# A fused LoRA linear layer on one core: the sixth chunk held back for the third store, and a self-test taken out

## The chip, the cores and the metric

The kernel runs on one core of one Trainium2 chip. The metric is the device time of one execution in microseconds (us); lower is better. A time is the median over several runs, and for this kernel 0.2% of it is 0.33 us. The profile shows one execution. Times inside it are microseconds from the start of its span. PE is TensorE (its weight loads are shown apart, as PEld), DVE is VectorE, ACT is ScalarE, POOL is GpSimd, SP is SyncE, which here only issues DMAs and waits.

## What is computed

`x` is 16 x 2048 x 256 in float32, so 32,768 rows of 256 values. `W` is 256 x 256, `lora_A` 256 x 16, `lora_B` 16 x 256, `lora_E` 16, `scale` is 1.

```python
y = x_flat @ W
lora_out = x_flat @ lora_A
lora_out = lora_out * lora_E
lora_out = lora_out @ lora_B
y = y + scale * lora_out
```

`x` is 33.55 MB, and so is the result. Both go through the core's 16 DMA engines once.

## The kernel before

The two low-rank factors are folded into the weight first: `weff = W + A E B`, a matrix of 256 x 256 in bf16 (lines 155 to 175). What is left is one product `x @ weff`.

**Chunks.** The rows are cut into nine chunks (`PLAN`, line 5), numbered 0 to 8: chunk 0 and chunk 6 have 16 rows per partition (2 MB), the others 32 rows (4 MB). There are six buffers in SBUF (`SLOTS`), and chunk i lives in buffer i mod 6. A chunk is loaded into its buffer, its result overwrites it there, and the buffer is stored to the output. So chunks 6, 7 and 8 use the buffers of chunks 0, 1 and 2 again.

**Steps.** Each chunk is worked off in steps of 8 rows per partition, 32 steps in all, t = 0 to 31. Chunk 0 is steps 0 and 1, chunk 1 is 2 to 5, chunk 2 is 6 to 9, chunk 3 is 10 to 13, chunk 4 is 14 to 17, chunk 5 is 18 to 21, chunk 6 is 22 and 23, chunk 7 is 24 to 27, chunk 8 is 28 to 31. A step goes through four engines' hands:

- DVE rounds the 8 rows to bf16 (`rounded(t)`, line 148; I write R(t)). Before the first step of a chunk it waits for that chunk's load (line 147).
- PE transposes them, two bf16 values as one 32-bit word (`transposed`, line 188; T(t)), into PSUM.
- DVE copies the transposed words to SBUF (`copied(t)`, line 152; C(t)).
- PE multiplies with `weff` (`multiplied`, line 197; M(t)), two groups of 4 rows, and ACT copies each group from PSUM over the input rows in the buffer (line 216).

**The order of each engine** is written out. DVE does R(0), R(1), and then C(t), R(t+2) for t = 0, 1, 2 and so on (lines 171 to 180). A DVE instruction that waits therefore holds up all behind it: R(18) stands between C(16) and C(17). PE does T(t+1), M(t) in a hardware loop (lines 205 to 208). ACT works in the order of the steps.

**The order of the DMAs** is that of SP. Ahead of everything come `W` and the loads of chunks 0 to 5 (lines 102 to 107). Then SP waits for each chunk in turn to be written by ACT, and issues its store (lines 224 and 225). After store 2 it issues loads 6, 7 and 8, each behind a wait until the store that used the same buffer (0, 1, 2) has landed (`AFTER`, lines 226 to 228). Store 3 is issued only behind load 8, then stores 4 to 8. ACT issues the three small loads of `lora_A`, `lora_B`, `lora_E`.

**The self-test** (lines 118 to 141) checks that a transpose of 32-bit words moves all bits unchanged: POOL makes two number patterns (`probe`, `want`), DVE shifts them, PE transposes one, DVE compares with the other and adds up the differences in `err`, which is 0. `err` is then added into `weff` (line 175), so `weff` waits for the test.

Of the kernel before, what the change touches and what calls it, by code (L numbers as in the profile page):

```python
# [7 lines left out]
LEAD = 6  # L8
AFTER = {2: [6, 7, 8]}

S, G = 8, 4
P = 128
FP32 = mybir.dt.float32
BF16 = mybir.dt.bfloat16
I32 = mybir.dt.int32


class Count:
# [12 lines left out]
def kernel(tc, x, W, lora_A, lora_B, lora_E, scale, out):  # L31
    nc = tc.nc
# [17 lines left out]
    def sbuf(name, shape, dt):  # L50
        return nc.alloc_sbuf_tensor(name, shape, dt).ap()

    def psum(name, shape, dt):
        return nc.alloc_psum_tensor(name, shape, dt).ap()
# [4 lines left out]
    w_sb = sbuf("w_sb", [P, KC, M], FP32)  # L59
# [3 lines left out]
    weff = sbuf("weff", [P, KC, M], BF16)  # L63
    ident = sbuf("ident", [P, P], FP32)
# [6 lines left out]
    ps_xt = [psum(f"psum_xt{k}", [P, S, P], FP32) for k in range(2)]  # L71
# [3 lines left out]
    ps_aeb = ps_xt[1][:, S // 2:, :].rearrange("p s t -> p (s t)").rearrange("p (c m) -> p c m", c=KC)  # L75

    s_w, s_a, s_b, s_e = (Count(nc, f"s_{k}") for k in "wabe")
    s_ld = [Count(nc, f"s_ld{i}") for i in range(len(PLAN))]
    s_st = [Count(nc, f"s_st{i}") for i in range(len(PLAN))]
    s_id, s_set, s_v, s_t, s_m, s_y = (  # L80
        Count(nc, k) for k in ("s_id", "s_set", "s_v", "s_t", "s_m", "s_y"))
# [3 lines left out]
    def slot(i):  # L85
        return slots[i % LEAD][:, :PLAN[i], :]
# [7 lines left out]
    def spent(engine, count):  # L94
        engine.wait_ge(count.sem, count.total).then_inc(count.sem, -count.total)
# [5 lines left out]
    with tc.tile_critical(no_gpsimd_drain=True):  # L101
# [12 lines left out]
        out=ident, in_=ident, compare_op=mybir.AluOpType.not_equal, fill=1.0, base=0,  # L114
        pattern=[[-1, P]], channel_multiplier=1))


    s_test = Count(nc, "s_test")
    probe = sbuf("probe", [P, P], I32)
    want = sbuf("want", [P, P], I32)  # L120
    got = sbuf("got", [P, P], FP32)
    s_test.by(nc.gpsimd.iota(probe, pattern=[[1, P]], base=0, channel_multiplier=P))
    s_test.by(nc.gpsimd.iota(want, pattern=[[P, P]], base=0, channel_multiplier=1))  # L123
    err = sbuf("err", [P, 1], FP32)
    A = mybir.AluOpType
    nc.vector.wait_ge(s_test.sem, 2)
    for t in (probe, want):
        s_test.by(nc.vector.tensor_scalar(out=t, in0=t, scalar1=16, scalar2=0x1235,  # L128
                                          op0=A.logical_shift_left, op1=A.bitwise_or))
    nc.tensor.wait_ge(s_test.sem, 4)  # L130
    nc.tensor.wait_ge(s_id.sem, 2)
    s_test.by(nc.tensor.transpose(ps_xt[0][:, 0, :], probe.bitcast(FP32), ident))  # L132
    nc.vector.wait_ge(s_test.sem, 5)
    s_test.by(nc.vector.tensor_copy(out=got, in_=ps_xt[0][:, 0, :]))  # L134
    nc.vector.wait_ge(s_test.sem, 6)
    s_test.by(nc.vector.tensor_tensor(out=want, in0=want, in1=got.bitcast(I32), op=A.bitwise_xor))  # L136
    nc.vector.wait_ge(s_test.sem, 7)
    s_test.by(nc.vector.tensor_scalar(out=got, in0=want, scalar1=0.0, scalar2=None, op0=A.not_equal))
    nc.vector.wait_ge(s_test.sem, 8)
    s_test.by(nc.vector.tensor_reduce(out=err, in_=got, axis=mybir.AxisListType.X, op=A.add))  # L140
    nc.tensor.wait_ge(s_test.sem, 6)


    def rounded(t):
        i, r = steps[t]
        if r == 0:
            nc.vector.wait_ge(s_ld[i].sem, 16)
        nc.vector.tensor_copy(out=xb[t % 2], in_=slot(i)[:, r:r + S, :]).then_inc(can_t, 1)  # L148

    def copied(t):  # L150
# [8 lines left out]
    for c in range(KC):  # L159
# [5 lines left out]
        out=ate, in0=ps_at, scalar1=e_sb, scalar2=float(scale),  # L165
        op0=mybir.AluOpType.mult, op1=mybir.AluOpType.mult))
    nc.tensor.wait_ge(s_v.sem, 2)
    for c in range(KC):
        aeb_done = nc.tensor.matmul(ps_aeb[:, c, :], ate[:, c, :], b_bf, start=True, stop=True)  # L169
    s_set.by(aeb_done)  # L170
    rounded(0)
    nc.vector.wait_ge(s_w.sem, 16)
    nc.vector.wait_ge(s_set.sem, 2)
    nc.vector.wait_ge(s_test.sem, 9)
    s_v.by(nc.vector.scalar_tensor_tensor(out=weff, in0=w_sb, scalar=err, in1=ps_aeb, op0=A.add, op1=A.add))  # L175
    rounded(1)
    for t in range(NS):
        copied(t)
        if t + 2 < NS:
            rounded(t + 2)  # L180
# [50 lines left out]
    for count in [s_a, s_id]:  # L231
        spent(nc.tensor, count)
    spent(nc.tensor, s_v)
    for count in [s_b, s_e, s_test, s_w, s_set, s_t] + s_ld:
        spent(nc.vector, count)
    spent(nc.scalar, s_m)
    nc.tensor.wait_ge(can_y, 1).then_inc(can_y, -1)
# [37 lines left out]
```

## Time and profile before

| | us |
|---|---|
| median of 3 runs | 163.13 (163.07 to 163.17) |
| the profiled execution, its own time | 162.98 |
| its span | 161.7 |
| outside the span | 1.3 |

| engine | busy us | share of the span | instructions |
|---|---|---|---|
| PE | 94.7 | 59% | 781 |
| PEld | 84.3 | 52% | 781 |
| DVE | 77.9 | 48% | 73 |
| ACT | 63.2 | 39% | 65 |
| POOL | 1.1 | 1% | 8 |

The DMA queue that SP feeds (q1) moved 67.37 MB, and its packets took 97.2% of the 16 engines' span. HBM was read for 33.85 MB and written for 33.55 MB, 417 GB/s over the span.

How to read it: a busy share is a mean over the whole span, and no compute engine is busy for more than 59% of it. What matters is which resource has no pause, and which of the waits in the order of SP and of DVE ends last. The profile has an answer that a page of shares does not print: the trace keeps a record of every DMA packet, with start, size and duration. For these big transfers a packet is 32,768 bytes (one partition of a 4 MB chunk) or 16,384 bytes (of a 2 MB chunk).

### The profile page before, as it was taken

To read this page: it belongs to the slowest core of one execution; us is meant where nothing else is said; L and a number is where in the kernel's file an instruction comes from. 1 tells how busy PE (TensorE), PEld (TensorE's weight loads), DVE (VectorE), ACT (ScalarE), POOL (GpSimd) and SP (SyncE) were. 2 spreads that over 40 slices of the span, in tenths; PEclk is the share of its full clock that TensorE was granted. 3 is DMA by queue.
4 is the path that set the end of the run, shared out by engine and by line. 5 is a ranking of instruction groups with operands and counts; after the bars stand their busy time and mean duration, and the time that the engine had idled before them with its cause. 6 is when DMAs were issued, how large, how long until landed. Compare 5 with 4: busy or idle time off the path is not lost. (4 is left out here: it accounts for less than half of the span.)

```text
span 161.7 us, 1984 instructions
## 1 busy us (share of the span) xinstructions
PE 94.7 (59%) x781; PEld 84.3 (52%) x781; DVE 77.9 (48%) x73; ACT 63.2 (39%) x65; POOL 1.1 (1%) x8
## 2 busy tenths in 40 slices
PE   0159399999999999994000895999995000000000
PEld 0037279999999999993000684999994000000000
DVE  0193297889898989860001907989840000000000
ACT  0300508686867767685000054677776000000000
POOL 0200000000000000000000000000000000000000
PEclk9999959999999999999755569999999655555555
DMA  4999999999999989999999999999999998999993
GB/s 138 430 454 454 414 430 454 422 422 454 422 430 446 399 341 446 454 446 397 462 385 450 462 438 399 454 438 397 478 422 405 462 438 381 478 438 397 462 438 146
DMA packets 2946, 67.42 MB, mean 417 GB/s; under 512 B 496, under 2 KB 512, under 8 KB 640
## 3 DMA queue, kind: packets, MB, share of 16 engines
q1 hardware_dynamic: 2736, 67.37, 97.2%
q10 hardware_dynamic: 208, 0.03, 0.2%
q14 instruction: 2, 0.02, 0.0%
HBM read 33.85 MB, written 33.55 MB: 417 GB/s over the span
## 5 line engine op out<-in xcount | busy, mean ns | idle before, releaser
L216 ACT COPY xy<-psum_y 128x1024 f32<-128x1024 f32 x64 | 61.9, 1017 | 55.8 <-PE psum_y L197 55.8
L197 PE MATMUL psum_y<-weff,xt 128*128 128x256 bf16 x512 | 64.9, 283 | 0.2 <-PEq L98 0.2
L197 PEld LDWEIGHTS psum_y<-weff,xt 128*128 128x128 bf16 x512 | 52.0, 102 | 7.7 <-issue 0.4
L148 DVE CAST xb<-xy 128x2048 bf16<-128x2048 f32 x32 | 39.0, 1219 | 27.3 <-DMA xy<-in_x_dram 27.3
L188 PE MATMUL psum_xt<-ident,xb 128*128 128x128 f32 x264 | 38.0, 293 | 20.2 <-PEq L98 20.2
L188 PEld LDWEIGHTS psum_xt<-ident,xb 128*128 128x128 f32 x264 | 32.9, 152 | 22.0 <-issue 21.6
L152 DVE COPY xt<-psum_xt 128x1024 f32<-128x1024 f32 x32 | 39.1, 1223 | 7.8 <-PE psum_xt L188 7.6
L132 PE MATMUL psum_xt<-ident,probe 128*128 128x128 f32 x1 | 0.5, 477 | 7.1 <-DVE want L128 7.1
L132 PEld LDWEIGHTS psum_xt<-ident,probe 128*128 128x128 f32 x1 | 0.2, 183 | 7.1 <-DVE want L128 7.1
L216 ACT ACT_TABLE_LOAD x1 | 1.3, 1283 | 5.7 <-PEq L109 5.7
L128 DVE TENSOR_SCALAR probe<-probe 128x128 int32<-128x128 int32 x1 | 0.2, 226 | 6.7 <-POOL want L123 6.7
L169 PE MATMUL psum_xt<-b_bf,ate 16*128 16x256 bf16 x2 | 0.6, 402 | 0.9 <-DVE ate L164 0.9
L169 PEld LDWEIGHTS psum_xt<-b_bf,ate 16*128 16x128 bf16 x2 | 0.1, 102 | 1.4 <-DVE ate L164 1.4
L160 PE MATMUL psum_xt<-ident,a_sb 128*16 128x128 f32 x2 | 0.6, 402 | 0.4 <-DVE got L134 0.4
L175 DVE SCALAR_TENSOR_TENSOR weff<-w_sb,err,psum_xt 128x512 bf16<-128x512 f32 x1 | 0.7, 742 | 0.0
L134 DVE COPY got<-psum_xt 128x128 f32<-128x128 f32 x1 | 0.3, 293 | 0.6 <-PE psum_xt L132 0.6
L164 DVE TENSOR_SCALAR ate<-psum_xt,e_sb 16x256 bf16<-16x256 f32 x1 | 0.5, 465 | 0.0
L160 PEld LDWEIGHTS psum_xt<-ident,a_sb 128*16 128x16 f32 x2 | 0.1, 92 | 0.7 <-DVE got L134 0.7
L136 DVE TENSOR_TENSOR want<-want,got 128x128 int32<-128x128 int32 x1 | 0.3, 292 | 0.0
L140 DVE TENSOR_REDUCE err<-got 128x1 f32<-128x128 f32 x1 | 0.3, 286 | 0.0
L113 POOL TENSOR_SCALAR_AFFINE_SELECT ident<-ident 128x128 f32<-128x128 f32 x1 | 0.3, 293 | 0.2 <-POOL ident L111 0.2
L156 DVE CAST b_bf<-b_sb 16x256 bf16<-16x256 f32 x1 | 0.3, 271 | 0.0
(9 smaller groups left out, 1.5 us busy)
## 6 DMA issues: line engine op xcount, KB each, us to landing
xy<-in_x_dram SPq DMA_DIRECT2D x7, 4096.0 KB, 26.6
out_dram<-xy SPq DMA_DIRECT2D x7, 4096.0 KB, 37.2
xy<-in_x_dram SPq DMA_DIRECT2D x2, 2048.0 KB, 16.1
out_dram<-xy SPq DMA_DIRECT2D x2, 2048.0 KB, 38.3
w_sb<-in_W_dram SPq DMA_DIRECT2D x1, 256.0 KB, 2.9
a_sb<-in_lora_A_dram ACTq DMA_DIRECT2D x1, 16.0 KB, 2.6
b_sb<-in_lora_B_dram ACTq DMA_DIRECT2D x1, 16.0 KB, 3.2
e_sb<-in_lora_E_dram ACTq DMA_DIRECT2D x1, 0.1 KB, 6.4
```

The source lines that it names most:

```text
L113: s_id.by(nc.gpsimd.affine_select(out=ident, in_=ident, compare_op=mybir.AluOpType.not_equal, fill=1.0, base=0, pattern=[[-1, P]], channel ...
L132: s_test.by(nc.tensor.transpose(ps_xt[0][:, 0, :], probe.bitcast(FP32), ident))
L134: s_test.by(nc.vector.tensor_copy(out=got, in_=ps_xt[0][:, 0, :]))
L148: nc.vector.tensor_copy(out=xb[t % 2], in_=slot(i)[:, r:r + S, :]).then_inc(can_t, 1)
L152: nc.vector.tensor_copy(out=xt[t % 2], in_=ps_xt[t % 2]).then_inc(can_m, 1)
L160: at_done = nc.tensor.transpose(ps_at[:, c, :], a_sb[:, c, :], ident)
L164: s_v.by(nc.vector.tensor_scalar(out=ate, in0=ps_at, scalar1=e_sb, scalar2=float(scale), op0=mybir.AluOpType.mult, op1=mybir.AluOpType.mult))
L169: aeb_done = nc.tensor.matmul(ps_aeb[:, c, :], ate[:, c, :], b_bf, start=True, stop=True)
L175: s_v.by(nc.vector.scalar_tensor_tensor(out=weff, in0=w_sb, scalar=err, in1=ps_aeb, op0=A.add, op1=A.add))
L188: done = nc.tensor.transpose(ps_xt[k][:, j, :], words[k][:, j, :], ident)
L197: done = nc.tensor.matmul(ps_y[h][:, j, :], pairs[k][:, h * G + j, :, c], weff[:, c, :], start=(c == 0), stop=(c == KC - 1))
L216: y = nc.scalar.copy(out=slot(i)[:, r:r + G, :], in_=ps_y[(n - 1) % 2])
```

## The change

It does two things.

1. `HOLD = {5: 2}`: before DVE rounds the first step of chunk 5 (that is R(18)), it waits, besides the load of chunk 5, until store 2 has landed.
2. The self-test is taken out: the two patterns on POOL, six instructions on DVE, one transpose on PE, and its semaphore. `weff` is now `W` plus the product, without `err`.

```diff
+HOLD = {5: 2}
...
-    s_test = Count(nc, "s_test")
-    probe = sbuf("probe", [P, P], I32)
-    want = sbuf("want", [P, P], I32)
-    got = sbuf("got", [P, P], FP32)
-    s_test.by(nc.gpsimd.iota(probe, ...))
-    s_test.by(nc.gpsimd.iota(want, ...))
...
-    for t in (probe, want):
-        s_test.by(nc.vector.tensor_scalar(out=t, in0=t, scalar1=16, scalar2=0x1235, ...))
...
-    s_test.by(nc.tensor.transpose(ps_xt[0][:, 0, :], probe.bitcast(FP32), ident))
...
-    s_test.by(nc.vector.tensor_copy(out=got, in_=ps_xt[0][:, 0, :]))
-    s_test.by(nc.vector.tensor_tensor(out=want, in0=want, in1=got.bitcast(I32), op=A.bitwise_xor))
-    s_test.by(nc.vector.tensor_scalar(out=got, in0=want, scalar1=0.0, scalar2=None, op0=A.not_equal))
-    s_test.by(nc.vector.tensor_reduce(out=err, in_=got, axis=mybir.AxisListType.X, op=A.add))
...
     def rounded(t):
         i, r = steps[t]
         if r == 0:
             nc.vector.wait_ge(s_ld[i].sem, 16)
+        if i in HOLD and r == 0:
+            nc.vector.wait_ge(s_st[HOLD[i]].sem, 16)
         nc.vector.tensor_copy(out=xb[t % 2], in_=slot(i)[:, r:r + S, :]).then_inc(can_t, 1)
...
-    nc.vector.wait_ge(s_test.sem, 9)
-    s_v.by(nc.vector.scalar_tensor_tensor(out=weff, in0=w_sb, scalar=err, in1=ps_aeb, op0=A.add, op1=A.add))
+    s_v.by(nc.vector.tensor_add(out=weff, in0=w_sb, in1=ps_aeb))
```

The order of the instructions on SP and ACT is the same in both kernels; on PE, DVE and POOL only the self-test's are missing, and the addition that makes `weff` is of another form.

More of the change, by code (lines that the diff above doesn't have):

```diff
@@ L14 @@
 BF16 = mybir.dt.bfloat16
-I32 = mybir.dt.int32
 class Count:
@@ L115 @@
         pattern=[[-1, P]], channel_multiplier=1))
-    s_test = Count(nc, "s_test")
-    probe = sbuf("probe", [P, P], I32)
-    want = sbuf("want", [P, P], I32)
-    got = sbuf("got", [P, P], FP32)
[L122 to L126, printed above, removed]
-    for t in (probe, want):
[L128 to L131, printed above, removed]
-    s_test.by(nc.tensor.transpose(ps_xt[0][:, 0, :], probe.bitcast(FP32), ident))
-    nc.vector.wait_ge(s_test.sem, 5)
-    s_test.by(nc.vector.tensor_copy(out=got, in_=ps_xt[0][:, 0, :]))
-    nc.vector.wait_ge(s_test.sem, 6)
-    s_test.by(nc.vector.tensor_tensor(out=want, in0=want, in1=got.bitcast(I32), op=A.bitwise_xor))
-    nc.vector.wait_ge(s_test.sem, 7)
-    s_test.by(nc.vector.tensor_scalar(out=got, in0=want, scalar1=0.0, scalar2=None, op0=A.not_equal))
-    nc.vector.wait_ge(s_test.sem, 8)
-    s_test.by(nc.vector.tensor_reduce(out=err, in_=got, axis=mybir.AxisListType.X, op=A.add))
-    nc.tensor.wait_ge(s_test.sem, 6)
     def rounded(t):
@@ L233 @@
     spent(nc.tensor, s_v)
-    for count in [s_b, s_e, s_test, s_w, s_set, s_t] + s_ld:
+    for count in [s_b, s_e, s_w, s_set, s_t] + s_ld:
         spent(nc.vector, count)
```

## The prediction, made before the changed kernel ran

> **What bounds the kernel now.** I read the slices of the page first, then SP's own waits, then the timeline, and last the packet records.
>
> ```profile
> PE   0159399999999999994000895999995000000000
> DVE  0193297889898989860001907989840000000000
> PEclk9999959999999999999755569999999655555555
> DMA  4999999999999989999999999999999998999993
> GB/s 138 430 454 454 414 430 454 422 422 454 422 430 446 399 341 446 454 446 397 462 385 450 462 438 399 454 438 397 478 422 405 462 438 381 478 438 397 462 438 146
> ```
>
> The DMA row has no pause from the second slice to the last but one. PE and DVE pause in slices 18 to 21, and from slice 31 on they do nothing. So the DMA engines set the end, although the chain of waits ends with ACT:
>
> ```profile
> 123.62 1.02 ACT xy L216
> ```
>
> Behind that copy, at 124.6, lie 37 us in which only stores run. The waits of SP tell that the transfers are a line, first in, first out:
>
> ```profile
> SPq L89 <- DMA out_dram<-xy: 35.3, 3, 16.8
> ...
> 64.12 19.63 SPq L89 DMA_DIRECT2D xy<-in_x_dram  x3
> 83.80 41.20 SPq L92 DMA_DIRECT2D out_dram<-xy  x6
> ```
>
> Load 6 is issued at 64.12, when store 0 has landed, and load 8 at 83.4, when store 2 has. By the records of the completion writes the landings are: load 5 59.3, stores 0 to 2 64.1, 73.8, 83.5, loads 6 to 8 88.4, 98.0, 107.8, stores 3 to 8 117.6, 127.7, 137.4, 142.3, 152.0, 161.6. Each transfer ends about 9.7 us (4 MB) or 4.9 us (2 MB) behind the one before, and the last landing is the end of the span.
>
> Then the packets. Of 1,792 packets of 32 KB, 1,650 took exactly 1,213 ns, and of 512 of 16 KB 466 took 611. Each DMA engine carries 112 and 32 of these: 135.9 + 19.6 = 155.4 us, with nothing lost. Joining each packet to the one that begins where it ended gives 16 unbroken chains, one per DMA engine. Fourteen end between 159.7 and 160.5, one at 161.03, one at 161.65. **The last one is the time.** Its packets over 1,213 ns, by stretch:
>
> ```
> stretch (us)    DMA does         compute runs   ns lost on the last chain / on the 14
> 10 - 53         loads            yes               9 / 5 to 25
> 53 - 57.9       end of load 5    yes             423 / 388 to 1308
> 57.9 - 76       stores 0, 1, 2   yes             821 / under 10
> 76 - 83.5       store 2          no              under 10 / under 10
> 83.5 - 106      loads 6, 7, 8    from 88         106 / under 20 (one 317)
> 106 - 126.5     stores 3, 4      to 124.6       1013 / under 10
> 126.5 - 161.6   stores 4 to 8    no              under 10 / under 10
> ```
>
> So one of 16 DMA engines is slower by some 72 ns in 1,213 (6%) whenever a store is moved while the compute engines run; not in loads, and not once they stop. It loses 0.82 + 1.01 us so, and comes in 0.62 us behind the next chain. That next one, at 161.03, lost about 1 us at the start and another at 57.0, where an 8 KB instruction fetch of 0.96 us lay between its packets.
>
> **The hold.** Before, R(18) began at 61.05; C(17) and all of chunk 5 went through by 75.8 (the last ACT copy there).
>
> ```profile
> 61.05 1.22 DVE L148 CAST xb<-xy 128x2048 bf16<-128x2048 f32 x1
> ...
> 63.40 1.93 ACT L216 COPY xy<-psum_y 128x1024 f32<-128x1024 f32 x2 [0.69 <-PE psum_y L197]
> ...
> 88.31 1.23 DVE L148 CAST xb<-xy 128x2048 bf16<-128x2048 f32 x1 [16.70 <-DMA xy<-in_x_dram]
> ```
>
> Now R(18) waits until store 2 lands, 83.5. Queued behind it on DVE is C(17), so step 17, the last of chunk 4, waits too, and store 4 with it. The last work ahead of the hold is step 16, whose ACT copies end at 63.40 + 1.93 = 65.3. Compute is silent from 65.3 to 83.5 in place of 75.8 to 88.3, and starts again just when loads 6 to 8 take over the DMA.
>
> *Saved under stores 0 to 2:* on the last chain the packets that begin at 65.5 and later lost 71, 61, 76, 71, 71, 71, 83 and 33 ns: 0.54 us.
>
> *Added under stores 3 and 4:* before, R(22) began cold at 88.31 and M(22) ended at 97.94. Moved to R(18) at 83.45, that is 4.86 us earlier and four steps back: M(18) ends at 93.08. From there the rows of the steady stretch give 2.62 us a step (0.87 of transposes and 1.75 of products, PE without a pause): M(31) ends at 93.08 + 13 x 2.62 = 127.1, and its copies 1.1 us later, 128.2, against 124.6. Loads 6 to 8 (88.4, 98.0, 107.8) are there before R(22), R(24), R(28) need them, at about 95, 100 and 111. So compute lies over the stores for 3.6 us more: 2.8 packets at 73 ns, the mean of the 13 whole packets there: 0.20 us.
>
> *The line of transfers:* step 17 done makes store 4 due at about 91, chunk 5's makes store 5 due at 102, store 6 at 107, store 7 at 118, store 8 at 128.2. The line reaches store 4 at 117.6, store 5 at 127.7 and store 8 at 152.0, so 24 us stay at the tightest, and order and bytes are unchanged. This backlog hides the later compute; without it each us of delay would be a us of time.
>
> *The sum:* -0.54 + 0.20 = -0.34 us on the last chain, which then ends at 161.3, still behind 161.03. What would be late next is that chain, so the hold can give 0.62 us at most.
>
> The Trainium skill speaks against this: "SBUF — State Buffer", section "SBUF: two separate sides", says engine ports and DMA ports are disjoint, and a DMA cannot be slowed by a compute op. The loads of 10 to 53 agree (1,213 ns under full compute); the 6% on one chain do not fit. By that rule they would come from elsewhere, and the hold would bring 0.
>
> **The self-test.** On DVE go 0.23 + 0.22 + 0.29 + 0.29 + 0.23 + 0.29 = 1.55 us, on PE one transpose of 0.48, on POOL 2 x 0.23. All of it runs between 6.3 and 8.9. R(0) began at 9.46, and load 0, issued at 1.38, takes 8.1 us (the shortest landing of L89): 9.5. So the load hides the test, and behind it R(2) waits 5.14 us for load 1 anyway. The plain addition has no row; it lies between 0.29 (a tensor op on 128 x 128) and 1.22 (a copy of 128 x 1024), and I take the 0.74 of the form that it replaces. The same wait hides each of them: 0. The bytes of W and x are the same. Fewer instructions can move the two fetches (57.0 and 100.5); they lie on two other chains, worth between 0 and 1 us there, and both end before 161.1. I take 0.
>
> **Result:** 162.98 - 0.34 = 162.64 on the profiled execution, and 163.13 - 0.34 = 162.8 on the median, which lies 0.15 above it.
>
> **The rivals.**
>
> 1. *No effect.* The 72 ns are not due to compute under stores, or are there only while the profile is recorded. For: it is one DMA engine of 16, while DVE, ACT and PE use all partitions alike, and records written for each instruction would stop with compute too. Against: the runs without its page take 163.07 to 163.17, not 0.6 us less than 162.98. Time: 163.13. This is what the page of the Trainium skill named above would give.
> 2. *The whole 0.54 and more.* If the extra 3.6 us cost nothing (the slow packets hang on an engine that is done early, as DVE is), the last chain falls to 161.1, to the limit of 161.03: 162.5 to 162.6.
> 3. *Slower by a bit.* The loss under stores 0 to 2 is of those stores and would come with an idle compute as well; then only the 0.20 remains. For: all of compute and those stores overlap, so the trace cannot part them. Against: 76 to 83.5, store 2 without compute, loses nothing. Time: 163.33, up to 163.5 if the continuous run costs twice as much a packet.
> 4. *Slower by much: the clock.* The granted clock was 0.5 from 78.9 to 96.0, and M(21) took 3.62 us cold against 1.91. My sum has as long a cold start (89.7 to 96.0, 6.3 us) from 84.8 on. Cold steps cost about 1.9 + 3.6 = 5.5 us, 2.9 more than warm. The 24 us of slack are used up by 8 more cold steps of the 14; each further one adds 2.9 us, and all 14 about 15 us: 178. Against: 26 steps in the trace run warm at 2.62 without a break.
>
> **How the numbers follow.** A measurement of this kernel tells about 0.2% (0.33 us) from no change, so the line for faster is 162.80 and my forecast lies on it; the price per packet (61 to 99 ns) and the end of compute (128.2 give or take 1) spread it from 162.6 to 163.0. Chances: forecast 0.62, of which 0.36 are beyond the line; no effect 0.17; rival 2 0.11; rival 3 0.07, of which 0.03 beyond 163.46; rival 4 0.03. Faster 0.36 + 0.11 = 0.47, slower 0.03 + 0.03 = 0.06, same 0.47. The range holds all but rival 4 and the outer ends: 162.4 to 163.35.
>
> **What would show it.** R(18) starts at 83.5, and DVE shows a wait of about 22 us for store 2 in place of 16.7 for load 6; ACT ends at about 128; SP issues store 4 at about 91 and store 5 at 102; on the last chain packets of 66 to 76 take 1,213 ns, and those of 106 to 129 some 1,285. Wrong if these stay slow while compute is silent, if slow packets appear under loads 6 to 8, or if a profile shows the 0.3 us and the runs do not.

## The result, and the profile after

The changed kernel takes 162.48 us (median of 11 runs, 162.40 to 162.91), against 163.05 before in the same series (162.87 to 163.29): a ratio of 0.9969, with an interval from 0.9960 to 0.9978. That is 0.51 us less (0.36 to 0.65). The profiled execution takes 162.47 with a span of 161.2, against 162.98 and 161.7.

The slices of the page, the same rows as before:

```profile
PE   0149089999999999000009999999999300000000
DVE  0164297898898982000049589899883000000000
PEclk9999969999999999955555899999999965555555
DMA  4999999999999989999999999999999998999993
```

The DMA row has the same digits as before. Counted from 0, the hole in PE and DVE has moved from slices 18 to 21 to slices 15 to 20, and behind it PE now runs on without the second dip that it had before. The end of the chain of waits and SP's issues:

```profile
126.40 1.02 ACT xy L192
```

```profile
63.50 19.67 SPq L90 DMA_DIRECT2D xy<-in_x_dram  x3
83.21 44.57 SPq L93 DMA_DIRECT2D out_dram<-xy  x6
```

Compute ends at 127.4 in place of 124.6, and the last store is issued 3 us later; 34 us of stores still follow, so that delay costs nothing. The hold itself, in DVE's timeline:

```profile
60.13 1.23 DVE L129 COPY xt<-psum_xt 128x1024 f32<-128x1024 f32 x1 [0.26 <-PE psum_xt L164]
82.92 1.23 DVE L125 CAST xb<-xy 128x2048 bf16<-128x2048 f32 x1 [21.57 <-DMA out_dram<-xy]
84.06 1.22 DVE L129 COPY xt<-psum_xt 128x1024 f32<-128x1024 f32 x1
```

The first row is C(16), the second R(18), released by a store's landing after 21.6 us, the third C(17), which had nothing left to wait for but its place in the line.

The packet records answer for the time. The chains are joined as in the prediction; the table has the ns lost over 1,213 (32 KB) and 611 (16 KB). All packet times, there and here, are set 0.50 us later than the trace has them, so that the last packet ends with the span.

```
                         before   after
last chain ends at       161.65   161.15
under stores 0 to 2         826     270
from store 3 on            1008    1260
the next chain ends at   161.03   160.61
```

After, two chains lie within 16 ns of each other from 65 to 106, so a join there can swap them; I count the two stretches as one DMA engine's, as in before. The landings bear it out: the slow chain ends store 4 at 127.74 before and at 127.20 after, each time when that store's last part lands (127.72 and 127.18 by the records of the completion writes, which are not shifted); what is lost behind it is under 0.05 us. The slow packets are still found only under stores beside compute, and on one DMA engine at a time. One line of the table is not of the hold: the chain at 161.03 had a fetch at 57.0; after, the two fetches lie at 88.2 and 105.3.

### The profile page after: what moved, and what is told of

The parts are those of the page before. It is cut to its first block, busy times and chain, and to the rows that moved or that the text cites. A ratio compares the mean times of both kernels' runs of the same rounds, so it can differ in the third digit from the quotient of the medians.

```text
span 161.2 us, 1973 instructions
## 1 busy us (share of the span) xinstructions
PE 92.5 (57%) x780; PEld 82.8 (51%) x780; DVE 76.8 (48%) x67; ACT 63.2 (39%) x65; POOL 0.7 (0%) x6
## 3 DMA queue, kind: packets, MB, share of 16 engines
q1 hardware_dynamic: 2736, 67.37, 97.6%
## 5 line engine op out<-in xcount | busy, mean ns | idle before, releaser
L173 PE MATMUL psum_y<-weff,xt 128*128 128x256 bf16 x512 | 64.2, 281 | 0.0
L173 PEld LDWEIGHTS psum_y<-weff,xt 128*128 128x128 bf16 x512 | 51.4, 101 | 7.4 <-issue 0.5
L125 DVE CAST xb<-xy 128x2048 bf16<-128x2048 f32 x32 | 39.0, 1218 | 28.1 <-DMA out_dram<-xy 21.6
L164 PE MATMUL psum_xt<-ident,xb 128*128 128x128 f32 x264 | 37.1, 288 | 26.2 <-PEq L99 26.2
L164 PEld LDWEIGHTS psum_xt<-ident,xb 128*128 128x128 f32 x264 | 32.1, 149 | 27.7 <-issue 27.3
L151 DVE TENSOR_TENSOR weff<-w_sb,psum_xt 128x512 bf16<-128x512 f32 x1 | 0.7, 681 | 0.0
```

Of the source, the lines that this page charges most:

```text
L151: s_v.by(nc.vector.tensor_add(out=weff, in0=w_sb, in1=ps_aeb))
L164: done = nc.tensor.transpose(ps_xt[k][:, j, :], words[k][:, j, :], ident)
L173: done = nc.tensor.matmul(ps_y[h][:, j, :], pairs[k][:, h * G + j, :, c], weff[:, c, :], start=(c == 0), stop=(c == KC - 1))
```

## Experiments

All of them compute what the kernel before computes; some do idle work beside it. Ratios are to the kernel before on the same chip.

### The two halves of the change

The hold alone, in the kernel before:

```diff
+HOLD = {5: 2}
...
+        if i in HOLD and r == 0:
+            nc.vector.wait_ge(s_st[HOLD[i]].sem, 16)
```

> The hold of chunk 5 for store 2 alone; the self-test stays. Theory A (one DMA engine loses some 72 ns a packet while stores run beside compute, and the hold takes compute off stores 0 to 2): 0.3 to 0.5 us less than the kernel before, the whole of what the change brought; on the last chain of packets 0.3 us lost under stores 0 to 2 and 1.25 under stores 3 and 4, against 0.83 and 1.01 before. Rival B (a part of the 0.51 us that the change brought, the 0.17 over my 0.34, is the missing self-test): 0.3 us less at most. Rival C (all of it is the self-test): the time of the kernel before.

Measured: 162.52 against 163.28, ratio 0.9950 (0.9930 to 0.9969). The packets beside compute lost 0.28 us under stores 0 to 2 and 1.27 from store 3 on.

The self-test out, without the hold:

```diff
-HOLD = {5: 2}
+HOLD = {}
```

> The self-test taken out, no hold. Theory A: the time of the kernel before within 0.1 us, R(0) still at 9.5 behind load 0, and the last chain loses 0.8 us under stores 0 to 2 and 1.0 under stores 3 and 4 as before. Rival B: some 0.17 us less. Rival C: some 0.5 us less.

Measured: 163.40 against 163.28, ratio 1.0005 (0.9993 to 1.0018), and 0.81 and 0.94 us lost. R(0) and what follows on DVE:

```profile
7.29 0.47 DVE L141 TENSOR_SCALAR ate<-psum_xt,e_sb 16x256 bf16<-16x256 f32 x1 [1.39 <-DMA e_sb<-in_lora_E_dram]
9.12 1.23 DVE L125 CAST xb<-xy 128x2048 bf16<-128x2048 f32 x1 [1.35 <-DMA xy<-in_x_dram]
10.26 0.68 DVE L151 TENSOR_TENSOR weff<-w_sb,psum_xt 128x512 bf16<-128x512 f32 x1
...
18.84 1.23 DVE L125 CAST xb<-xy 128x2048 bf16<-128x2048 f32 x1 [5.14 <-DMA xy<-in_x_dram]
```

The front of the kernel now waits 1.35 us for load 0, which the test filled before, and then 5.14 us for load 1, as before. The plain addition took 0.68 us. So the whole gain is the hold's; rivals B and C fall.

### Holding more, and holding for another store

```diff
-HOLD = {5: 2}
+HOLD = {4: 2}
```

> Self-test out, and chunk 4 instead of chunk 5 waits for store 2, so four steps more are held. Theory A: compute is silent from about 55 to 83, nothing is lost under stores 0 to 2 (0.83 before), but compute then ends at about 138 in place of 124.6, and 13.3 us more of it under stores cost 10.4 packets at 73 ns, 0.76 us: together 0.06 us less than the kernel before, so within 0.15 of it, and 0.2 to 0.4 us more than the changed kernel. A rival by which the hold helps through the silence itself (31 us of it rather than 18) expects less time than the changed kernel.

Measured: 162.89 against 163.28, ratio 0.9971 (0.9956 to 0.9986): 0.47 us less than before (0.23 to 0.72), where 0.06 was expected. By the medians it is 0.37 us longer than the hold of chunk 5 alone in the same series; 0.2 to 0.4 over the changed kernel was expected. Nothing was lost under stores 0 to 2, and 1.72 us under stores 3 to 6; compute ended at 137.9.

```diff
-HOLD = {5: 2}
+HOLD = {5: 1}
```

> Self-test out, and chunk 5 waits for store 1 (landing at 73.8) instead of store 2. Compute pauses from 65 to 74 and then runs beside store 2, waits for load 6 at 88 and goes on as before. Theory A: nothing is gained, since the loss moves from 65 to 76 to 74 to 84: 0.8 us on the last chain under stores 0 to 2 and 1.0 under stores 3 and 4, the time of the kernel before within 0.1 us. A rival by which any hold of chunk 5 helps expects some 0.3 us less.

Measured: 163.04, ratio 0.9986 (0.9974 to 0.9998), 0.23 us less (0.03 to 0.42), where nothing was expected. R(18) ran at 72.94, when store 1 had landed:

```profile
72.94 1.23 DVE L125 CAST xb<-xy 128x2048 bf16<-128x2048 f32 x1 [12.28 <-DMA out_dram<-xy]
...
79.67 1.22 DVE L129 COPY xt<-psum_xt 128x1024 f32<-128x1024 f32 x1 [0.97 <-PE psum_xt L164]
...
87.87 1.23 DVE L125 CAST xb<-xy 128x2048 bf16<-128x2048 f32 x1 [4.35 <-DMA xy<-in_x_dram]
```

Here the packets are slow from 75.2 to 81.5, beside the compute that has come back, and not between 64 and 75, where it is silent though store 1 is moved. That answers rival 3 of the prediction, which the trace of before could not: the loss goes with compute, not with stores 0 to 2. The sum was 0.56 + 1.10 us. My expectation had overlooked that the restart is cold (DVE waits 0.97 us for PE at 79.67), so that fewer instructions fall beside store 2: 126 end between 72.9 and 82.4, for 349 ns lost there, 2.8 ns each. By the medians the order of the four is the expected one (chunk 5 for store 2 the best, then chunk 4, then store 1, then no hold), but the intervals of neighbours overlap, and the packets of the two profiles (1.72 and 1.66 us) do not put chunk 4 ahead of store 1. A long silence for its own sake is not seen to bring anything, as the run that holds chunk 4 is not the fastest. The sizes of the last two are some 0.2 to 0.4 us more than expected.

### Which work makes the packets slow

Four kernels put idle work of one engine behind the end of compute, beside stores 4 to 6, each as in this one, with its own instruction in the place of the copy:

```diff
+    s_d = Count(nc, "s_d")
+    for d in range(20):
+        if d:
+            nc.scalar.wait_ge(s_d.sem, d)
+        s_d.by(nc.scalar.copy(out=xt[0].rearrange(...), in_=ps_y[0]))
+    spent(nc.scalar, s_d)
```

> The changed kernel with 20 idle copies of ACT behind its last one (128 x 1024 from PSUM to a free buffer, each waiting for the one before), so ACT alone runs for some 22 us beside stores 4 to 6, which before had no compute beside them. Question: which engine makes the packets of one DMA engine slow. If ACT's work on its own does it, some 17 packets between 127 and 149 take 1,285 ns instead of 1,213, 1.2 us in all, and the span is longer by as much (162.4 against 161.2). If it is the number of instructions that counts (0.9 a us here, against some 20 a us in the real steps, nearly all PE's), nothing happens: 1,213 ns and 161.2.

> The same with 18 idle copies of DVE (128 x 1024 from PSUM to a free buffer), some 23 us of DVE alone beside stores 4 to 6. If DVE's work on its own makes one DMA engine slow: some 18 packets of 1,285 ns, 1.3 us longer. If the number of instructions counts: nothing.

> The same with 60 idle copies of DVE of an eighth of the size (128 x 128), some 20 us with 3 instructions a us instead of 0.8. If DVE's busy time makes packets slow, as many are slow as in the run with large copies; if it is the number of instructions, the loss a packet is some four times that of the large copies, and a sixth of the 72 ns of the real steps, some 12 ns.

> The same with 192 idle transposes of PE into a PSUM buffer that nobody reads any more, some 21 us of PE alone beside stores 4 to 6, with 18 matmuls and weight loads a us as in the real steps. If PE (its reads, or its many instructions) makes packets slow: some 16 packets of 1,285 ns, 1.2 us longer, span 162.4. If ACT's writes over the buffers are needed: 1,213 ns and 161.2.

The idle work in the timelines of the ACT and of the large DVE run, and the groups of the PE run:

```profile
126.66 20.87 ACT L217 COPY xt<-psum_y 128x1024 f32<-128x1024 f32 x20
```

```profile
124.40 22.61 DVE L216 COPY xt<-psum_xt 128x1024 f32<-128x1024 f32 x18 [2.51 <-DVEq L96]
```

```profile
L216 PEld LDWEIGHTS psum_xt<-ident,xb x192: 139/140/142, 125.9 to 146.7; 128*128 128x128 f32 x192
L216 PE MATMUL psum_xt<-ident,xb x192: 272/273/301, 125.9 to 146.8; 128*128 128x128 f32 x192
```

Each was run once, so the packets tell more than the spans (161.8, 161.4, 161.5, 162.2, where the changed kernel's lie between 161.1 and 161.6). From 128 on, once the real steps are over:

```
idle work              instructions a us   a slow packet   lost in all
ACT, 20 large copies          0.9           13 to 14 ns, one packet in four      0.06 us
DVE, 18 large copies          0.8           13 to 14 ns, one packet in four      0.05 to 0.08
DVE, 60 small copies          3             9 to 23 ns, most packets             0.16
PE, 192 transposes           18             42 to 61 ns, all of 32 KB            0.82
real steps                   20             49 to 108 ns, all of 32 KB           1.0 to 1.3
```

ACT and DVE were busy nearly all the time in the first two, as much as in the real steps or more, and lost next to nothing. The loss goes by the number of instructions: 55 ns over 20 copies is 2.8 ns each, 156 over some 50 is 3.1, 822 over 358 matmuls and weight loads is 2.3, and the real steps lose 72 ns in 1.285 us, 147 in a step of 2.62 us with 52 instructions, 2.8 each. (The PE run's four packets of 324 to 412 ns, beside fetches of its longer program, are left out.) Semaphores are not the cause: the 192 idle transposes increment none.

### The count of instructions, on the clock

POOL has nothing to do in the middle of the kernel. 256 tiny memsets there move next to no data:

```diff
+    nc.gpsimd.wait_ge(s_st[0].sem, 16)
+    with nc.gpsimd.Fori(0, 32):
+        for d in range(8):
+            nc.gpsimd.memset(idle[:, d:d + 1], 0.0).then_inc(s_d, 1)
+        nc.gpsimd.wait_ge(s_d, 8).then_inc(s_d, -8)
```

> The changed kernel, with 256 tiny memsets on POOL, which is idle there, once store 0 has landed (64): they move next to no data, and run while chunk 5 is held and stores 1 and 2 are moved. Theory A2 (the loss goes by the number of instructions, some 2.8 ns each, whichever engine carries them out: 147 ns lost in a step of 2.62 us with 52 instructions, 14 ns a packet with 3 instructions a us on DVE, some 55 with 18 a us on PE): 256 x 2.8 = 0.7 us more than the changed kernel, so the gain of the hold is eaten up; on the last chain 0.5 to 0.8 us are lost between 64 and 83. Rival A1 (the loss comes of the data that the compute engines move): the time of the changed kernel.

The other run waits for `s_ld[1]`, the landing of load 1, instead.

> The same 256 memsets on POOL, but started when load 1 has landed (19), beside loads 2 to 4. Theory A2: loads are not slowed by it, as they are not by the real steps; the time of the changed kernel within 0.1 us. A rival by which the memsets cost time in themselves (a longer program, POOL's port) expects the same loss as in the run with stores.

And the changed kernel beside them:

> The changed kernel once more, beside the next two on one chip, because its gain came out at 0.51 us (0.36 to 0.65) and that of the hold alone at 0.8 (0.5 to 1.1), over the 0.34 that I had worked out. If 0.34 is right: 0.3 to 0.4 us less than the kernel before; if a second gain lies beside it: 0.5 to 0.8.

Measured against 163.17 of before: the changed kernel 162.64 (0.9967, 0.9955 to 0.9979); with the memsets beside stores 1 and 2, 163.65 (1.0031, 1.0019 to 1.0043), **1.01 us more** than without; with the memsets beside loads, 162.78 (0.9976, 0.9964 to 0.9988), whose interval overlaps that of the changed kernel. The tile of the memsets in the first, and a stretch of POOL's timeline in the second:

```profile
L124 POOL MEMSET idle<- x256: 98/99/1036, 63.5 to 86.4; 128x1 f32 x128
```

```profile
19.11 1.22 POOL L124 MEMSET idle<- 128x1 f32 x8 [12.86 <-DMA xy<-in_x_dram]
20.81 0.33 POOL L124 MEMSET idle<- 128x1 f32 x8 [0.48 <-POOLq L125]
```

In the first, R(18) stayed where it was (83.7, after 22.5 us of waiting), and the last chain lost 1.02 us between 64.5 and 83.6, on every packet, 42 to 94 ns, where the changed kernel loses next to nothing (0.03): the whole of the 1.01. In this stretch lie 28 of the 32 rounds of the loop; the last four run beside load 6. That is 36.4 ns for a round; with its wait, its register step and its branch beside the eight memsets, 11 instructions at 3.3 ns. I had counted the memsets alone, hence 0.7. Beside loads, the same instructions slowed no packet.

### Another cut of the chunks

```diff
-PLAN = [16] + [32] * 5 + [16, 32, 32]
-SLOTS = [16, 32, 32, 32, 32, 32]
-LEAD = 6
-AFTER = {2: [6, 7, 8]}
-HOLD = {5: 2}
+PLAN = [16, 16] + [32] * 4 + [16, 16, 16, 32, 16]
+SLOTS = [16, 16, 32, 32, 32, 32, 16]
+LEAD = 7
+AFTER = {3: [7, 8, 9, 10]}
+HOLD = {6: 3}
```

> The changed kernel with other chunks: the second one has 2 MB instead of 4, so that compute goes on at 14 instead of 19, a last small chunk closes the first group of loads, and that chunk 6 waits for store 3, the last store ahead of the second group of loads. So 13 steps are left for the time after the hold instead of 15, and the second group of loads (24.3 us) covers more of them. Theory A2: compute beside stores falls from 27 us (58 to 65.4 and 107.8 to 127.4) to some 20 (58 to 63.5 and 111.6 to 126), 0.3 to 0.4 us less than the changed kernel, 0.8 to 0.9 less than the kernel before. A rival by which only the hold's silence counts expects the time of the changed kernel; if two more loads and stores cost something in themselves, it is slower than that.

Measured: 163.00 against 163.31, ratio 0.9977 (0.9965 to 0.9990); not faster than the changed kernel. DVE's and ACT's timelines show where compute went otherwise than I had reckoned:

```profile
23.81 1.23 DVE L125 CAST xb<-xy 128x2048 bf16<-128x2048 f32 x1 [5.08 <-DMA xy<-in_x_dram]
...
93.30 1.23 DVE L125 CAST xb<-xy 128x2048 bf16<-128x2048 f32 x1 [0.75 <-DMA xy<-in_x_dram]
...
102.83 1.23 DVE L129 COPY xt<-psum_xt 128x1024 f32<-128x1024 f32 x1 [0.26 <-PE psum_xt L164]
107.87 1.23 DVE L125 CAST xb<-xy 128x2048 bf16<-128x2048 f32 x1 [3.81 <-DMA xy<-in_x_dram]
```

```profile
68.06 1.93 ACT L192 COPY xy<-psum_y 128x1024 f32<-128x1024 f32 x2 [0.69 <-PE psum_y L173]
```

Compute went on at 14.1, but then waited for the next load until 23.8, and the work ahead of the hold ended at 70.0 instead of 63.5. The 4 MB chunk among the late loads landed only at 107.9, so compute stood still under loads, where its silence saves nothing, and ended at 130.9 instead of 126. I had reckoned the steps one behind the other and not set each against its load. The changed kernel has no such pause under its late loads. So the slow packets still cost 1.39 us, against 1.53 in the changed kernel. And the cut has a price of its own: from one start to the next, an undisturbed packet of 16 KB takes 608.2 ns and one of 32 KB 1,210.1, and each DMA engine has 64 of the small ones in the place of 32 large ones, some 0.20 us by estimate. That is the last rival of the expectation, and somewhat more than the smaller loss saved.

## Why the prediction was right

**The bound** was right: the DMA line kept its order and its backlog, and the last chain of packets ended with the span in both kernels.

**The term under stores 0 to 2** was forecast at -0.54 us and measured at -0.56 (826 to 270 ns). **The term under stores 3 and 4** was forecast at +0.20 and measured at +0.25: compute ended at 127.4, 0.8 before the 128.2 of my sum, while the packets from 108 to 126 lost about 76 ns each rather than 73. The 0.8 is there from the start: R(18) began at 82.92 and not 83.45, since store 2 landed earlier, and the cold stretch was shorter (84.3 to 89.5, 5.2 us, where I had 6.3), so M(18) ended at 92.27 and not 93.08. M(17) took 3.62 us cold as forecast, and the steady step 2.62.

**The self-test** was forecast at 0, hidden by loads 0 and 1, and the run without it alone gave a ratio of 1.0005 with 1 inside the interval.

**The size** is where it fell short. The two terms give -0.31 in the pair of profiles and -0.34 in the forecast; the runs gave -0.51 (0.36 to 0.65), -0.54 in the second series (0.34 to 0.73) and -0.82 for the hold alone (0.51 to 1.14). The forecast lies just outside the first and the last of these and at the edge of the second. The sum of losses beside compute under stores, over all chains, is 1.95 and 1.75 us in the two profiles without a hold and 1.63, 1.53 and 1.55 in those of the same hold, a mean of 0.28 between them. What the rest is, some 0.2 us, stays open. It isn't the self-test. The start of the chains and the end of load 5 cost the chains between 88 and 1,308 ns there, unevenly from run to run, but they lie ahead of the hold; one profile a kernel can't part a small shift of these from chance.

**The rivals.** *No effect* fell, with the reason that I gave for it half right: tiny memsets on POOL slow the packets as much as real work, so it is not the data that engines move in SBUF. The rule of the Trainium skill ("SBUF — State Buffer", "SBUF: two separate sides"), that a DMA cannot be slowed by a compute op, is therefore not refuted for its ports: loads under full compute took 1,213 ns, and so did three in four store packets beside large copies. But as a forecast of time it failed here by 0.51 us, since instructions did slow a DMA engine, by a way that the runs do not name. *The whole 0.54*, with a floor at 161.03, gave the closest time (162.5) for a reason that did not hold: the 3.6 us of added overlap did cost (0.25). *Slower by a bit* fell with the hold for store 1, where the packets beside stores are fast in the silence and slow after it. *The clock* fell: the steps ran cold for 5.2 us, with a granted clock of 0.5 until 89.5, and then at 2.62. (The 78.9 and 96.0 of the prediction carry the same shift as its packets; the trace has 78.4 and 95.5.)

**What the slow packets are** is settled only in part. Shown: they come with instructions of any engine (PE, DVE and POOL clearly, ACT barely), some 2.3 to 3.3 ns for each, on one DMA engine, in stores and not in loads; what the instruction moves matters little, and a semaphore that it increments is not needed. Argued, and not shown: that it is the writing of the record that the profile keeps of each instruction. My argument against this in the prediction was void: every run here, the timed ones too, lists a span and a granted clock, so all of them were recorded. A run without records wasn't tried, and whether the 0.51 us are there in one stays open.

## What to carry to other kernels

When the DMA line has no pause, compare the packets of all DMA engines before calling it full: one slow engine of 16 sets the end, and the page's mean hides it (97.2% and 97.6% here). Where stores slow down beside instructions and loads don't, put the idle time of compute under the stores: the hold costs nothing as long as the backlog of transfers (24 us here) is longer than the delay. And since such a loss can be of the recording itself, a gain of this size should be looked for once without it.

## What the runs showed of the hardware that I had not expected

- 256 memsets of 128 x 1 on an idle engine, beside stores, cost 1.01 us in a kernel that has nothing to do with them; beside loads, 0.14 us by the medians, with overlapping intervals.
- 20 copies of 128 x 1024 on ACT, 21 us of work beside stores, cost one DMA engine 0.06 us; 192 transposes on PE, 21 us as well, 0.82 us.
- An instruction fetch of 8 KB is carried by one DMA engine between the packets of the big transfers (0.31 us, 0.96 in the stretch at 57.0), and the packet behind it takes 169 to 582 ns longer (72 behind the one at 57.0).
